# Attention scores of two 64-deep heads: one zero-padded product before, two products on the TensorE array's two halves after

## Chip, cores, metric

The kernel runs on one core of a Trainium2 chip. The metric is the device time of one execution in microseconds (us). A core has five engines: TensorE (PE in the profile; PEld is its weight loads), VectorE (DVE), ScalarE (ACT), GpSimd (POOL) and SyncE (SP), which here only issues DMAs.

## What is computed

Two decoder layers over 256 tokens of width 1024, in float32. Each layer has an attention mixer, a squared-ReLU MLP of hidden width 4096 and a gated embedding. Layer 0 mixes with 8 stick-breaking heads and 4 differential heads (each with two score maps, so also two 64-deep products); layer 1 with 16 heads of block attention, which at 256 tokens is plain causal attention. All heads are 64 deep. Of the scores the reference says, in short:

```
z = einsum('bhqd,bhkd->bhqk', q, k) * scale      # d = 64, q and k: 256 tokens
stick:  w = exp(log_sigmoid(z) + sum of log_sigmoid(-z) over later keys), s < t
diff:   a = softmax(q1 k1) - lam * softmax(q2 k2), causal
layer 1: softmax(q k), causal
```

## The kernel before

Weights stream from HBM. Each unit of 128 x 1024 floats lands in a `raw` buffer, ACT writes its rounded part (`whi`), DVE the rest (`wlo = raw - whi`), and a product of two float32 matrices is three products of the rounded type fp32r: hi x hi, hi x lo, lo x hi (`mm3`). A pair (`whi`, `wlo`) is one of `N_SPLIT` = 6 split buffers, which a chunk gives back when PE has read it. PE works on blocks of 128 tokens (t = 0, 1) by 512 columns, or of 128 columns by 256 tokens (`chunk_T`, `ff1`).

The order of all instructions is written out by a planner in the kernel (class `Order`): tasks are generators with a rank, and the planner picks by rank among those whose inputs are ready by its own clock. The engines then run their lists in order. The trunk (projections, MLP, gate) has rank 80, heads 21 and 22, and the small projection `ple_projection` (products `whi,pT`) has rank 90 and fills in when the trunk has nothing ready; it starts after all scores of its layer (`scored`).

The heads are handled in pairs j of two 64-deep heads, head g on partitions 64g to 64g+63: 4 `stick_pair`, 4 `diff_head`, 8 `moba_pair`. One operand lies in a padded tile (`z` for hi, `zl` for lo) with room for both heads, in which the other head's 64 partitions are zero. A product then contracts over all 128 partitions and yields the scores of both heads side by side. `z_tile` sets the zeros with GpSimd memsets (L1195, L1196): 8 at the start, 4 in layer 1. `qk_sink` and `T_sink` write the two halves of padded tiles with two 64-partition instructions each. For a softmax pair, `soft` computes block t = 0 (128 keys of each head: 256 columns) and later block t = 1 (512 columns). `stick_pair` adds a mask by a bf16 product and sums the logarithms with constants `negl` and `negone`. `average` multiplies by the values in the array's two column halves (`mm_halves`, L165). A head pair holds two of the `N_BIG` = 5 buffers `big` (a stick pair one).

Time is also spent in `transposes` after each residual: transpose on PE, copy by ACT (`tok`), cast and subtraction by DVE (`T0h`, `T0l`), which the next projection reads.

Of the kernel before, what the change touches and what calls it, by code (L numbers as in the profile page):

```python
# [17 lines left out]
P = 128  # L18
# [8 lines left out]
N_SPLIT = 6  # L27
N_RAW = 4
N_BIG = 5
# [11 lines left out]
def width(ap):  # L41
    n = 1
    for s in ap.shape[1:]:
        n *= int(s)
    return n
# [37 lines left out]
class Order:  # L83
# [84 lines left out]

    def transpose(self, out, in_, ident):
        self.nc.tensor.transpose(out, in_, ident)  # L170
        return self.spend("pe", 109)
# [56 lines left out]
def kernel(  # L228
# [25 lines left out]
    NT = 8  # L254
# [348 lines left out]
    def qk_sink(nm, dst, ev, eighth, padded):  # L603
        def sink(t, bk, dep):
            yield (dep, toks.wake, nm.ev[t])
            ti, tok = toks.take()
            rs = nm.rs8 if eighth else nm.rs
            e = o.copy(tok, bk[1], ps=True, scale=rs[:, t:t + 1])
            banks.give(*bk, e)
            yield (e, rope_ev, ropes.wake)  # L610
            ri, r = ropes.take()
            v = tok.rearrange("q (h d) -> q h d", d=64)
            c16 = cc[:, t].rearrange("q a b -> q (a b)").unsqueeze(1).to_broadcast([P, 8, 16])
            o.tt_pool(r[:, 0], v[:, :, 0:16], c16, ALU.mult)
            o.tt_pool(r[:, 1, :, 0:8], v[:, :, 8:16], sn[:, t, 0, :].unsqueeze(1).to_broadcast([P, 8, 8]), ALU.mult)
# [11 lines left out]
            ts_ = slice(t * P, (t + 1) * P)  # L627
# [7 lines left out]
            for v, (hi, lo) in parts:  # L635
                e = o.tt(lo, v, hi.bitcast(F32), ALU.subtract)
            banks.give(bi, ps, e, side=True)
            ev[t].t = e
        return sink
# [15 lines left out]
    def T_sink(dst, evs_, eighth, padded):  # L655
        def sink(f2, bk, dep):
            yield (dep, toks.wake, rsT_ev)
            ti, tok = toks.take()
            v = tok.rearrange("q (j n) -> q j n", j=2)
            ps = bk[1].rearrange("q (j n) -> q j n", j=2)  # L660
            e = o.stt(v, ps, 0.125 if eighth else 1.0, rsT.unsqueeze(1).to_broadcast([P, 2, 256]), ALU.mult, ALU.mult)
            banks.give(*bk, e)
            yield e
            js = slice(2 * f2, 2 * f2 + 2)
            if padded:
                parts = [(v[64 * g:64 * g + 64], [d[64 * g:64 * g + 64, js, g, :] for d in dst]) for g in range(2)]
            else:
                parts = [(v, [d[:, js, :] for d in dst])]
            for v_, (hi, lo) in parts:
                e = o.act(hi, v_, AF.Copy)  # L670
            yield e
            for v_, (hi, lo) in parts:
                e = o.tt(lo, v_, hi.bitcast(F32), ALU.subtract)
            toks.give(ti, tok, e)
            evs_[f2].t = e
        return sink
# [49 lines left out]
    def stick_pair(j, kT, qz, q_ev, k_ev, v, v_ev, acts):  # L726
        yield (q_ev[j // 2], k_ev[j // 2], mask_ev, big.wake)
        b1 = big.take()
        e = b1[1]
        yield lambda: banks.wake(2, side=True)  # L730
        ba, bb = banks.take(side=True), banks.take(side=True)
        pa, pb = ba[1], bb[1][:, :256]
        a3 = pa.rearrange("q (g n) -> q g n", g=2)
        b3 = pb.rearrange("q (g n) -> q g n", g=2)
# [5 lines left out]
        yield ea  # L740
        o.act(e[:, :512], pa, AF.Abs, ps=True)
        o.act(e[:, 512:], pb, AF.Abs, ps=True, dep=eb)
        o.act(e, e, AF.Exp, scale=-1.0)
        t = o.act(e, e, AF.Ln, bias=one)
        yield t
        o.stt(e[:, 512:], pb, 0.0, e[:, 512:], ALU.max, ALU.add)
        t = o.stt(e[:, :512], pa, 0.0, e[:, :512], ALU.max, ALU.add)
# [3 lines left out]
        t = o.act(sph, e, AF.Copy)  # L751
        yield t
        t = o.tt(spl, e, sph.bitcast(F32), ALU.subtract)
# [6 lines left out]
        sps.give(*b2, t2)  # L760
        yield t1
        t1 = o.act(e[:, :512], pa, AF.Exp, ps=True)
        t2 = o.act(e[:, 512:], pb, AF.Exp, ps=True)
        banks.give(*ba, t1, side=True)
        banks.give(*bb, t2, side=True)
        yield (t2, *v_ev)
        wa = e[:, :512].rearrange("q (g n) -> q g n", g=2)
        wb = e[:, 512:].rearrange("q (g n) -> q g n", g=2)
        yield from average(lambda g: wa[:, g, :], lambda g: wb[:, g, :], v, j * P, acts, j, b1)


    def soft(j, t, qT, kz, q_ev, k_ev, e, st):

        n = (t + 1) * P
        yield (q_ev[t], *k_ev[:t + 1], mask_ev)
        yield lambda: banks.wake(side=True)
        bs = banks.take(side=True)
        s3 = bs[1][:, :2 * n].rearrange("q (g k) -> q g k", g=2)
        ts_ = slice(t * P, (t + 1) * P)
        w = mm3(s3, qT[0][:, j, ts_], qT[1][:, j, ts_], kz[0][:, j, :, 0:n], kz[1][:, j, :, 0:n], True, True)  # L780
        if t == 1:
            scored()
        yield w
        for g in range(2):

            nc.vector.tensor_tensor_reduce(e[:, g, :], s3[:, g, :], cmask[:, P * (1 - t):], -1.0, 3.0e38, ALU.add, ALU.min,
                                           accum_out=st[:, g:g + 1])
            w = o.spend("dve", 130 + 1.04 * n)
        banks.give(*bs, w, side=True)
# [9 lines left out]
    def diff_head(j, qT, kz, q_ev, k_ev, v, v_ev, acts):  # L799
# [3 lines left out]
        w = 0.0  # L803
        es = []
        for t in range(2):
            e = be[1][:, 256 * t:256 * t + 256 * (t + 1)].rearrange("q (g k) -> q g k", g=2)
            st = sts[t][1]
            w = yield from soft(j, t, qT, kz, q_ev, k_ev, e, st)
# [42 lines left out]
    def moba_pair(j, jj, qT, kz, q_ev, k_ev, v, v_ev, acts):  # L851
# [4 lines left out]
        aT = ba[1].rearrange("q (g a n) -> q g a n", g=2, a=3)  # L856
        for t in range(2):
# [3 lines left out]
            yield from soft(j, t, qT, kz, q_ev, k_ev, e, st)  # L861
# [327 lines left out]
    def z_tile(name, layer, j):  # L1189

        z = zpool.tile([P, 4, 2, 256], F32R, tag="z", name=name)
        def zeros():
            yield o.now if layer else 1500.0
            for y in (z, zl[j]) if layer == 0 else (z,):
                nc.gpsimd.memset(y[64:128, :, 0, :].bitcast(F32), 0.0)  # L1195
                nc.gpsimd.memset(y[0:64, :, 1, :].bitcast(F32), 0.0)  # L1196
                o.spend("pool", 1800)
        o.add(zeros(), 14)
        return z, zl[j]
# [7 lines left out]
    def trunk():  # L1207
# [6 lines left out]
        for i in range(2):  # L1214
            banks.room[0] += 5 - banks.room[0] if i == 0 else 1
            z = [z_tile(f"z{i}{j}", i, j) for j in range(2)]
# [8 lines left out]
            if i == 0:  # L1225
                o.add(p_task(0, pT_ev, 40000.0), 40)
                sinks = dict(bq=qk_sink(nm, sT[1], evs["bq"], True, False),
                             bk=qk_sink(nm, z[1], evs["bk"], False, True),
                             aq=T_sink(z[0], evs["aq"], True, True),
                             ak=T_sink(sT[0], evs["ak"], False, False),  # L1230
# [10 lines left out]
            else:  # L1241
                o.add(p_task(1, pT_ev, o.now), 40)
                for n, _ in ORDER1:
                    g = int(n[1])
                    s = dict(q=lambda: qk_sink(nm, sT[g], evs[n], True, False),
                             k=lambda: qk_sink(nm, z[g], evs[n], False, True),
# [53 lines left out]
```

## Time and profile before

| | us |
|---|---|
| three runs | 670.27, 670.45, 671.4 (median 670.45) |
| the profiled execution | 671.49, of it 669.7 the span of the trace |
| PE busy | 654.9 |
| DVE, ACT, POOL busy | 450.3, 417.2, 63.8 |

A busy PE is counted from the start of a product to its modelled end. Products overlap, so what one costs is read from the distance to the next, not from its length.

### The profile page before, as it was taken

How to read it: one execution, taken by the hardware profiler on the slowest of the kernel's cores; microseconds unless marked ns; L12 is line 12 of the kernel's file. 1: busy time of each engine (PE TensorE's matmuls, PEld its weight loads, DVE VectorE, ACT ScalarE, POOL GpSimd, SP SyncE). 2: the span in 40 equal slices, each digit the busy share in tenths (PEclk: the TensorE clock that was granted, in tenths of full speed). 3: DMA queues.
4: the chain of work that ended last, by engine and by line, in shares of the span. 5: the costliest groups of instructions: out<-in, count | busy, mean ns of one | idle time of the engine just before them, and what ended most of it. 6: DMA issues, size and time to landing. Idle time of an engine off the chain costs nothing.

```text
span 669.7 us, 10988 instructions
## 1 busy us (share of the span) xinstructions
PE 654.9 (98%) x3906; PEld 572.0 (85%) x3906; DVE 450.3 (67%) x935; ACT 417.2 (62%) x888; POOL 63.8 (10%) x128
## 2 busy tenths in 40 slices
PE   6999999999999999999999999998999999999995
PEld 5899778898998899888888778777998999899885
DVE  6799867766645754577986866747656555655594
ACT  6777986756544644466796767756646543655483
POOL 8650001000000000000052022000000000000010
PEclk9999999999999999999999999999999999999998
DMA  7853733456447544753566434416466546754621
GB/s 255 263 165 106 240 127 112 138 188 213 158 168 252 191 154 159 251 198 120 187 210 187 153 126 136 149 63 189 154 225 218 167 152 218 224 165 156 209 95 63
DMA packets 50054, 115.61 MB, mean 173 GB/s; under 512 B 4000, under 2 KB 5456, under 8 KB 50000
## 3 DMA queue, kind: packets, MB, share of 16 engines
q1 hardware_dynamic: 49824, 114.39, 52.5%
q8 instruction: 30, 0.49, 0.3%
q0 software_dynamic: 176, 0.53, 0.2%
q14 instruction: 24, 0.20, 0.1%
HBM read 113.86 MB, written 1.05 MB: 172 GB/s over the span
## 4 chain that ended last, share of the span: by engine, by line
PE 91%; DVE 3%; POOL 2%; issue 1%; DMA 1%; ACT 1%; SPq 0%; POOLq 0%; DVEq 0%; ACTq 0%
PE bank L159 86%; PE bank L170 3%; DVE wlo L192 2%; PE bank L165 1%; DMA raw<-in_ab_w_in_dram 1%; POOL prod L1110 1%; POOL rem L1111 0%; ACT junk L178 0%; ACT whi L178 0%; DVE h L192 0%; DVE T0h L510 0%; DVE T0l L192 0%; ACT tok L178 0%; POOL negr L312 0%; DVE o L192 0%
## 5 line engine op out<-in xcount | busy, mean ns | idle before, releaser
L192 DVE TENSOR_TENSOR wlo<-raw,whi 128x512 fp32r<-128x512 f32 x424 | 277.1, 694 | 91.4 <-ACT whi L178 65.7
L178 ACT ACTIVATE whi<-raw 128x512 fp32r<-128x512 f32 x424 | 243.7, 626 | 92.7 <-PE bank L159 67.4
L159 PE MATMUL bank<-T0h,whi 128*128 128x256 f32 x576 | 162.8, 283 | 1.7 <-DVE T0h L510 1.7
L159 PE MATMUL bank<-T0h,wlo 128*128 128x256 f32 x576 | 162.3, 282 | 0.3 <-DVE wlo L192 0.2
L159 PE MATMUL bank<-T0l,whi 128*128 128x256 f32 x576 | 162.2, 282 | 0.2
L159 PE MATMUL bank<-whi,hid 128*128 128x512 f32 x512 | 160.9, 390 | 0.0
L159 PEld LDWEIGHTS bank<-whi,hid 128*128 128x128 f32 x512 | 96.1, 188 | 19.2
L159 PEld LDWEIGHTS bank<-T0h,wlo 128*128 128x128 f32 x576 | 110.2, 191 | 0.9 <-DVE wlo L192 0.9
L159 PEld LDWEIGHTS bank<-T0h,whi 128*128 128x128 f32 x576 | 108.3, 188 | 2.8 <-DVE T0h L510 2.1
L159 PEld LDWEIGHTS bank<-T0l,whi 128*128 128x128 f32 x576 | 108.6, 189 | 1.4 <-DVE T0l L192 0.8
L159 PE MATMUL bank<-wlo,hid 128*128 128x512 f32 x256 | 99.6, 389 | 0.0
L192 DVE TENSOR_TENSOR tok<-tok 128x512 f32<-128x512 f32 x32 | 22.1, 690 | 68.3 <-ACT tok L178 68.3
L159 PE MATMUL bank<-whi,T0h 128*128 128x512 f32 x160 | 66.2, 413 | 0.0
L178 ACT ACTIVATE tok<-bank 128x512 f32<-128x512 f32 x32 | 18.8, 586 | 72.4 <-PE bank L159 72.4
L159 PE MATMUL bank<-wlo,T0h 128*128 128x512 f32 x160 | 63.2, 395 | 0.0
L159 PE MATMUL bank<-whi,T0l 128*128 128x512 f32 x160 | 63.1, 394 | 0.0
L159 PEld LDWEIGHTS bank<-wlo,hid 128*128 128x128 f32 x256 | 48.1, 188 | 9.3
L159 PE MATMUL bank<-whi,T1h 128*128 128x512 f32 (+1 forms) x136 | 53.6, 394 | 0.0
L159 PE MATMUL bank<-whi,T1l 128*128 128x512 f32 (+1 forms) x136 | 51.5, 379 | 0.0
L159 PE MATMUL bank<-wlo,T1h 128*128 128x512 f32 (+1 forms) x136 | 51.4, 378 | 0.0
L534 POOL TENSOR_TENSOR rs_p<-ms_p,pexp 128x1 f32<-128x1 f32 x4 | 2.2, 551 | 437.0 <-DVE ms_p L209 437.0
L159 PEld LDWEIGHTS bank<-whi,T0l 128*128 128x128 f32 x160 | 30.3, 190 | 6.6
(159 smaller groups left out, 742.6 us busy)
## 6 DMA issues: line engine op xcount, KB each, us to landing
raw<-in_w_ff_dram SPq DMA_DIRECT2D x128, 512.0 KB, 4.4
raw<-in_moba_w_in_dram SPq DMA_DIRECT2D x24, 512.0 KB, 4.0
raw<-in_ab_w_in_dram SPq DMA_DIRECT2D x23, 512.0 KB, 4.8
raw<-in_ple_gate_dram SPq DMA_DIRECT2D x16, 512.0 KB, 4.7
raw<-in_ab_w_out_dram SPq DMA_DIRECT2D x8, 512.0 KB, 4.1
raw<-in_moba_w_out_dram SPq DMA_DIRECT2D x8, 512.0 KB, 3.3
raw<-in_ple_proj_dram SPq DMA_DIRECT2D x4, 512.0 KB, 3.8
h<-in_x_dram SPq DMA_DIRECT2D x4, 256.0 KB, 5.8
```

The costliest lines, as they stand in the source:

```text
L159: self.nc.tensor.matmul(out, lhsT, rhs, start=start, stop=stop, **kw)
L165: self.nc.tensor.matmul(out, lhsT, rhs, start=start, stop=stop)
L170: self.nc.tensor.transpose(out, in_, ident)
L178: self.nc.scalar.activation(out, in_, func, **kw)
L192: self.nc.vector.tensor_tensor(out, a, b, op=op)
L534: nc.gpsimd.tensor_tensor(nm.rs[:, t:t + 1], b, pexp[:, 0:1], op=ALU.pow)
L1110: nc.gpsimd.tensor_scalar(prod, k, -c, None, op0=ALU.mult)
```

## The change

The padding goes. q and k of a pair lie in unpadded tiles of 128 partitions, and each head's scores are a product over its own 64 partitions, issued alternately for g = 0 and g = 1 into two PSUM banks (`mm3_heads`). For softmax pairs both blocks t are now computed in one go (`scores_of`), into two banks that are held together, and then read by DVE together (`read_scores`). The stick pair's mask and log sums are issued per head. The memsets and the second half of each padded write are gone. Freed room goes to a seventh split buffer, two more `big`, and eight more `tiny`.

```
-N_SPLIT = 6
+N_SPLIT = 7
 N_RAW = 4
-N_BIG = 5
+N_BIG = 7
...
+    def mm3_heads(self, steps, first=True):
+
+        for a, b, start, stop in ((0, 0, first, False), (0, 1, False, False), (1, 0, False, True)):
+            for out, l_, r_ in steps:
+                self.nc.tensor.matmul(out, l_[a], r_[b], start=start, stop=stop, skip_group_check=not first)
...
-    NT = 8
+    NT = 16
...
-            if padded:
-                parts = [(v[64 * g:64 * g + 64], [d[64 * g:64 * g + 64, :, g, ts_] for d in dst]) for g in range(2)]
-            else:
-                parts = [(v, [d[:, :, ts_] for d in dst])]
-            for v, (hi, lo) in parts:
-                e = o.act(hi, v, AF.Copy, ps=True)
+            hi, lo = [d[:, :, t * P:(t + 1) * P] for d in dst]
+            e = o.act(hi, v, AF.Copy, ps=True)
...
+    def head_rows(x, j, g, c0, c1):
+
+        return [d[64 * g:64 * g + 64, j, c0:c1] for d in x]
...
-        mm3(a3, kT[0][:, j, 0:P], kT[1][:, j, 0:P], qz[0][:, j, :, :], qz[1][:, j, :, :], True, False)
-        ea = o.mm(a3[:, :, 0:P], identb, smask, False, True)
-        mm3(b3, kT[0][:, j, P:256], kT[1][:, j, P:256], qz[0][:, j, :, P:256], qz[1][:, j, :, P:256], True, False)
-        eb = o.mm(b3, identb, smask, False, True)
...
+        o.mm3_heads([(ps[g][:, :256], head_rows(kT, j, g, 0, P), head_rows(q, j, g, 0, 256)) for g in range(2)])
+        o.mm3_heads([(ps[g][:, 256:384], head_rows(kT, j, g, P, 256), head_rows(q, j, g, P, 256)) for g in range(2)],
+                    first=False)
+        ws = []
+        for g in range(2):
+            for c in (0, 256):
+                w = o.mm(ps[g][:, c:c + P], identb, smask[:, 0], False, True, skip_group_check=True)
...
-        for s_ in (sph, spl):
-            o.mm(pa, negl, s_[:, :512], False, False, skip_group_check=True)
-            t1 = o.mm(a3[:, :, P:256], negone, s_[:, 512:].rearrange("q (g n) -> q g n", g=2), False, s_ is spl,
-                      skip_group_check=True)
-            t2 = o.mm(pb, negl, s_[:, 512:], False, s_ is spl, skip_group_check=True)
...
+        for g in range(2):
+            for s_ in (sph, spl):
+                sg = s_.rearrange("q (g n) -> q g n", g=2)[:, g]
+                o.mm(ps[g][:, :384], negl, sg, False, False, skip_group_check=True)
+                w = o.mm(ps[g][:, P:256], negone, sg[:, 256:384], False, s_ is spl, skip_group_check=True)
...
+    def scores_of(j, q, k, q_ev, k_ev):
+
+        yield (*q_ev, *k_ev, mask_ev)
+        yield lambda: banks.wake(2, side=True)
+        bs = [banks.take(side=True) for _ in range(2)]
+        ws = [o.mm3_heads([(bs[g][1][:, P * t:P * t + P * (t + 1)], head_rows(q, j, g, P * t, P * (t + 1)),
+                            head_rows(k, j, g, 0, P * (t + 1))) for g in range(2)]) for t in range(2)]
+        scored()
+        return bs, ws
...
-    def z_tile(name, layer, j):
-
-        z = zpool.tile([P, 4, 2, 256], F32R, tag="z", name=name)
-        def zeros():
-            yield o.now if layer else 1500.0
-            for y in (z, zl[j]) if layer == 0 else (z,):
-                nc.gpsimd.memset(y[64:128, :, 0, :].bitcast(F32), 0.0)
-                nc.gpsimd.memset(y[0:64, :, 1, :].bitcast(F32), 0.0)
...
+        z = zpool.tile([P, 2, 4, 256], F32R, tag="z", name=name)
+        return z[:, 0], z[:, 1]
...
-    zl = [cst.tile([P, 4, 2, 256], F32R, name=f"zl{j}") for j in range(2)]
```

## Rows read from the trace of the kernel before

**Rows 1.** The page: span, busy time of engines, and the chain that ended last.
```profile
span 669.7 us, 10988 instructions
PE 654.9 (98%) x3906; PEld 572.0 (85%) x3906; DVE 450.3 (67%) x935; ACT 417.2 (62%) x888; POOL 63.8 (10%) x128
PE 91%; DVE 3%; POOL 2%; issue 1%; DMA 1%; ACT 1%; SPq 0%; POOLq 0%; DVEq 0%; ACTq 0%
```
**Rows 2.** PE in order of time, two softmax pairs (start, length, instruction).
```profile
45.32 0.28 PE L159 MATMUL bank<-z,sT 128*128 128x256 f32 x1
...
46.03 0.28 PE L159 MATMUL bank<-T0h,whi 128*128 128x256 f32 x1
...
48.91 0.40 PE L159 MATMUL bank<-z,sT 128*128 128x512 f32 x1
...
49.61 0.28 PE L159 MATMUL bank<-T0h,whi 128*128 128x256 f32 x1
```
**Rows 3.** PE in order of time, a stick pair's mask and its log sums.
```profile
62.01 0.28 PE L159 MATMUL bank<-smask,identb 128*128 128x256 bf16 x1
...
80.41 0.64 PE L159 MATMUL bank<-sph,negr 128*128 128x512 f32 x3
80.89 0.63 PE L159 MATMUL bank<-spl,negr 128*128 128x512 f32 x3
```
**Rows 4.** PE in order of time, an average in column halves, from three narrow windows.
```profile
81.24 0.28 PE L159 MATMUL bank<-spl,negr 128*128 128x256 f32 x1
81.45 0.44 PE L165 MATMUL bank<-big,v 128*64 128x256 f32 x2
...
81.45 0.65 PE L165 MATMUL bank<-big,v 128*64 128x256 f32 x4
...
81.45 0.87 PE L165 MATMUL bank<-big,v 128*64 128x256 f32 x8
82.25 0.50 PE L159 MATMUL bank<-whi,T0h 128*128 128x512 f32 x1
```
**Rows 5.** Weight loads by line and shape (busy us, mean ns of one).
```profile
L159 PEld LDWEIGHTS bank<-z,sT 128*128 128x128 f32 x32 | 6.1, 190 | 1.4 <-issue 0.5 <-DVE big L209 0.2
L165 PEld LDWEIGHTS bank<-big,v 128*64 128x64 f32 x96 | 5.8, 136 | 5.2 <-issue 1.2 <-ACT whi L178 1.1 <-ACT big L178 0.7
L159 PEld LDWEIGHTS <-identb 128*128 128x128 bf16 x8 | 0.8, 95 | 1.3 <-issue 1.1
```
**Rows 6.** PE in order of time, float32 products of 128 columns.
```profile
99.22 2.17 PE L159 MATMUL bank<-v,big 128*128 128x128 f32 x18
```
**Rows 7.** PE in order of time, first products of layer 1's MLP, with idle time.
```profile
457.64 0.28 PE L159 MATMUL bank<-T0h,whi 128*128 128x256 f32 x1
...
459.93 0.38 PE L159 MATMUL bank<-T0h,whi 128*128 128x256 f32 x1 [1.22 <-DVE T0h L510]
...
463.07 0.28 PE L159 MATMUL bank<-T0h,wlo 128*128 128x256 f32 x1
```
**Rows 8.** DVE in order of time, ahead of that stretch.
```profile
443.95 0.42 DVE L192 TENSOR_TENSOR T1l<-bank,T1h 128x256 fp32r<-128x256 f32 x1 [3.65 <-ACT T1h L178]
```
**Rows 9.** Products that read pT, by stretch: layer 1, then layer 0.
```profile
443.00:446.00 3.00, 2.34 (x9) 1.61 (x9) 0.00 (x0) 0.00 (x0) 1.00 0.04 14
...
127.00:129.50 2.50, 2.04 (x9) 1.69 (x9) 0.00 (x0) 0.00 (x0) 1.00 0.63 176
```
**Rows 10.** The start: GpSimd, then DVE casts by shape, ACT, PE.
```profile
9.63 0.94 POOL L1196 MEMSET zl<- 64x1024 f32 x1
...
L510 DVE CAST T0h<-tok 128x256 fp32r<-128x256 f32 x3 | 2.4, 804 | 0.3 <-ACT tok L178 0.3
...
30.44 0.22 ACT L178 ACTIVATE sh<-rem 128x16 f32<-128x16 f32 x1 [1.28 <-POOL rem L1111]
...
36.87 0.28 PE L159 MATMUL bank<-T0l,whi 128*128 128x256 f32 x1
...
38.27 0.28 PE L159 MATMUL bank<-T0h,whi 128*128 128x256 f32 x1
```

More of the change, by code (lines that the diff above doesn't have):

```diff
@@ L167, in mm_halves @@
         return e
+    def mm3_heads(self, steps, first=True):
+        for a, b, start, stop in ((0, 0, first, False), (0, 1, False, False), (1, 0, False, True)):
+            for out, l_, r_ in steps:
+                self.nc.tensor.matmul(out, l_[a], r_[b], start=start, stop=stop, skip_group_check=not first)
+                e = self.spend("pe", max(0.5 * width(r_[b]) / 2.4, 55.0) + 6)
+        return e
     def transpose(self, out, in_, ident):
@@ L601, with qk_sink @@
     rope_ev = Event()
-    def qk_sink(nm, dst, ev, eighth, padded):
+    def qk_sink(nm, dst, ev, eighth):
         def sink(t, bk, dep):
@@ L626, in sink @@
             v = ps.rearrange("q (j n) -> q j n", j=4)
-            ts_ = slice(t * P, (t + 1) * P)
-            if padded:
-                parts = [(v[64 * g:64 * g + 64], [d[64 * g:64 * g + 64, :, g, ts_] for d in dst]) for g in range(2)]
-            else:
-                parts = [(v, [d[:, :, ts_] for d in dst])]
-            for v, (hi, lo) in parts:
-                e = o.act(hi, v, AF.Copy, ps=True)
+            hi, lo = [d[:, :, t * P:(t + 1) * P] for d in dst]
+            e = o.act(hi, v, AF.Copy, ps=True)
             yield e
-            for v, (hi, lo) in parts:
-                e = o.tt(lo, v, hi.bitcast(F32), ALU.subtract)
+            e = o.tt(lo, v, hi.bitcast(F32), ALU.subtract)
             banks.give(bi, ps, e, side=True)
@@ L653, in rows_task, with T_sink @@
         banks.give(bi, ps, rsT_ev.t, side=True)
-    def T_sink(dst, evs_, eighth, padded):
+    def T_sink(dst, evs_, eighth):
         def sink(f2, bk, dep):
@@ L663, in sink @@
             yield e
[L664 to L670, printed above, removed]
+            hi, lo = [d[:, 2 * f2:2 * f2 + 2, :] for d in dst]
+            e = o.act(hi, v, AF.Copy)
             yield e
-            for v_, (hi, lo) in parts:
-                e = o.tt(lo, v_, hi.bitcast(F32), ALU.subtract)
+            e = o.tt(lo, v, hi.bitcast(F32), ALU.subtract)
             toks.give(ti, tok, e)
@@ L724, in scored, with stick_pair @@
             scores[1].t = o.now
-    def stick_pair(j, kT, qz, q_ev, k_ev, v, v_ev, acts):
+    def head_rows(x, j, g, c0, c1):
+        return [d[64 * g:64 * g + 64, j, c0:c1] for d in x]
+    def stick_pair(j, kT, q, q_ev, k_ev, v, v_ev, acts):
         yield (q_ev[j // 2], k_ev[j // 2], mask_ev, big.wake)
         b1 = big.take()
-        e = b1[1]
+        e = b1[1].rearrange("q (g n) -> q g n", g=2)
         yield lambda: banks.wake(2, side=True)
[L731 to L734, printed above, removed]
-        mm3(a3, kT[0][:, j, 0:P], kT[1][:, j, 0:P], qz[0][:, j, :, :], qz[1][:, j, :, :], True, False)
-        ea = o.mm(a3[:, :, 0:P], identb, smask, False, True)
-        mm3(b3, kT[0][:, j, P:256], kT[1][:, j, P:256], qz[0][:, j, :, P:256], qz[1][:, j, :, P:256], True, False)
-        eb = o.mm(b3, identb, smask, False, True)
-        scored()
[L740 to L744, printed above, removed]
+        bs = [banks.take(side=True) for _ in range(2)]
+        ps = [b[1] for b in bs]
+        o.mm3_heads([(ps[g][:, :256], head_rows(kT, j, g, 0, P), head_rows(q, j, g, 0, 256)) for g in range(2)])
[5 more added lines that the diff above has]
+                w = o.mm(ps[g][:, c:c + P], identb, smask[:, 0], False, True, skip_group_check=True)
+            ws.append(w)
+        scored()
+        yield ws[0]
+        for g in range(2):
+            o.act(e[:, g], ps[g][:, :384], AF.Abs, ps=True, dep=ws[g])
+        o.act(b1[1], b1[1], AF.Exp, scale=-1.0)
+        t = o.act(b1[1], b1[1], AF.Ln, bias=one)
         yield t
-        o.stt(e[:, 512:], pb, 0.0, e[:, 512:], ALU.max, ALU.add)
-        t = o.stt(e[:, :512], pa, 0.0, e[:, :512], ALU.max, ALU.add)
+        for g in range(2):
+            t = o.stt(e[:, g], ps[g][:, :384], 0.0, e[:, g], ALU.max, ALU.add)
         yield (t, sps.wake)
@@ L760, in stick_pair @@
[L760 to L783, printed above, removed]
-        for g in range(2):
[L786 to L789, printed above, removed]
@@ new lines, in stick_pair @@
+        ws = []
+        for g in range(2):
+            for s_ in (sph, spl):
+                sg = s_.rearrange("q (g n) -> q g n", g=2)[:, g]
+                o.mm(ps[g][:, :384], negl, sg, False, False, skip_group_check=True)
+                w = o.mm(ps[g][:, P:256], negone, sg[:, 256:384], False, s_ is spl, skip_group_check=True)
+            ws.append(w)
+        sps.give(*b2, w)
+        yield ws[0]
+        for g in range(2):
+            t = o.act(e[:, g], ps[g][:, :384], AF.Exp, ps=True, dep=ws[g])
+            banks.give(*bs[g], t, side=True)
@@ new lines, in stick_pair, with halves_of @@
+        yield (t, *v_ev)
+        yield from average(lambda g: e[:, g, :256], lambda g: e[:, g, 256:], v, j * P, acts, j, b1)
+    def halves_of(b):
+        return [b[:, 256 * t:256 * t + 256 * (t + 1)].rearrange("q (g k) -> q g k", g=2) for t in range(2)]
+    def scores_of(j, q, k, q_ev, k_ev):
+        yield (*q_ev, *k_ev, mask_ev)
+        yield lambda: banks.wake(2, side=True)
+        bs = [banks.take(side=True) for _ in range(2)]
+        ws = [o.mm3_heads([(bs[g][1][:, P * t:P * t + P * (t + 1)], head_rows(q, j, g, P * t, P * (t + 1)),
+                            head_rows(k, j, g, 0, P * (t + 1))) for g in range(2)]) for t in range(2)]
+        scored()
+        return bs, ws
@@ new lines, in read_scores @@
+    def read_scores(bs, ws, es, sts):
+        yield ws[1]
+        ends = []
+        for t in range(2):
+            n = (t + 1) * P
+            for g in range(2):
+                nc.vector.tensor_tensor_reduce(es[t][:, g, :], bs[g][1][:, P * t:P * t + n], cmask[:, P * (1 - t):], -1.0, 3.0e38,
+                                               ALU.add, ALU.min, accum_out=sts[t][:, g:g + 1])
+                w = o.spend("dve", 130 + 1.04 * n)
+            ends.append(w)
+        for b in bs:
+            banks.give(*b, w, side=True)
+        return ends
@@ L790, in soft @@
+    def soft(w, e, st):
         yield w
@@ L802, in diff_head @@
         sts = [tinies.take(), tinies.take()]
-        w = 0.0
         es = []
+        bs, ws = yield from scores_of(j, qT, kz, q_ev, k_ev)
+        ends = yield from read_scores(bs, ws, halves_of(be[1]), [x[1] for x in sts])
         for t in range(2):
@@ L807, in diff_head @@
             st = sts[t][1]
-            w = yield from soft(j, t, qT, kz, q_ev, k_ev, e, st)
+            w = yield from soft(ends[t], e, st)
             yield lam_ev
@@ L856, in moba_pair @@
         aT = ba[1].rearrange("q (g a n) -> q g a n", g=2, a=3)
+        bs, ws = yield from scores_of(j, qT, kz, q_ev, k_ev)
+        ends = yield from read_scores(bs, ws, halves_of(be[1]), [x[1] for x in sts])
         for t in range(2):
@@ L860, in moba_pair @@
             e = be[1][:, 256 * t:256 * t + n].rearrange("q (g k) -> q g k", g=2)
-            yield from soft(j, t, qT, kz, q_ev, k_ev, e, st)
+            yield from soft(ends[t], e, st)
             for g in range(2):
@@ L1187, in p_task, with z_tile @@
         pT_ev.t = e
-    def z_tile(name, layer, j):
-        z = zpool.tile([P, 4, 2, 256], F32R, tag="z", name=name)
-        def zeros():
-            yield o.now if layer else 1500.0
-            for y in (z, zl[j]) if layer == 0 else (z,):
-                nc.gpsimd.memset(y[64:128, :, 0, :].bitcast(F32), 0.0)
-                nc.gpsimd.memset(y[0:64, :, 1, :].bitcast(F32), 0.0)
-                o.spend("pool", 1800)
-        o.add(zeros(), 14)
-        return z, zl[j]
+    def z_tile(name):
+        z = zpool.tile([P, 2, 4, 256], F32R, tag="z", name=name)
+        return z[:, 0], z[:, 1]
     sl = [cst.tile([P, 4, 256], F32R, name=f"sl{j}") for j in range(2)]
-    zl = [cst.tile([P, 4, 2, 256], F32R, name=f"zl{j}") for j in range(2)]
     cst.tile([P, 80], F32, name="room")
@@ L1215, in trunk @@
             banks.room[0] += 5 - banks.room[0] if i == 0 else 1
-            z = [z_tile(f"z{i}{j}", i, j) for j in range(2)]
+            z = [z_tile(f"z{i}{j}") for j in range(2)]
             v = vpool.tile([P, 2, D], F32, tag="v", name=f"v{i}")
@@ L1226, in trunk @@
                 o.add(p_task(0, pT_ev, 40000.0), 40)
[L1227 to L1230, printed above, removed]
+                sinks = dict(bq=qk_sink(nm, sT[1], evs["bq"], True),
+                             bk=qk_sink(nm, z[1], evs["bk"], False),
+                             aq=T_sink(z[0], evs["aq"], True),
+                             ak=T_sink(sT[0], evs["ak"], False),
                              av=v_sink(nm, v, 0, evs["av"]), bv=v_sink(nm, v, 512, evs["bv"]))
@@ L1244, in trunk @@
                     g = int(n[1])
-                    s = dict(q=lambda: qk_sink(nm, sT[g], evs[n], True, False),
-                             k=lambda: qk_sink(nm, z[g], evs[n], False, True),
+                    s = dict(q=lambda: qk_sink(nm, sT[g], evs[n], True),
+                             k=lambda: qk_sink(nm, z[g], evs[n], False),
                              v=lambda: v_sink(nm, v, 512 * g, evs[n]))[n[0]]()
```

4 lines of the change are left out of this document (2 added, 2 removed).

## The prediction

> **What bounds the kernel now.** I read the page first: PE is busy for 654.9 of 669.7 us and makes 91% of the chain that ended last [rows 1]. The other engines have slack on average, so an edit on DVE, ACT, POOL or in the DMA stream pays only where PE stands still. I then read PE in order of time for what one product costs. Six score products of 256 columns take from 45.32 to 46.03, 0.118 each, and three of 512 columns from 48.91 to 49.61, 0.233 each, to the next product's start [rows 2]. The lengths (0.28 and 0.40) are latency and are not added up. Next, over the same order of time, I looked for places where the distance between products exceeds these prices. After the first 15 us there are few that this change can reach. One is at 457.64 to 463.07, the beginning of layer 1's MLP: 21 products start there, 20 steps that need 2.36 us take 5.43, so 3.1 us are lost, and the row in the middle waits 1.22 for DVE's `T0h` [rows 7]. The other is at 36.87 to 38.27: 5 steps, 0.59 needed, 1.40 taken, 0.8 lost [rows 10]. The reader is to see that everything but PE's own work is worth at most some 5 us here, and that the change moves PE's own work by terms of the same size.
>
> **Softmax pairs, on PE.** There are 12 (4 and 8). Before, a pair costs 3 x 0.118 + 3 x 0.233 = 1.05 us [rows 2]. After, block t = 1 is three duos (one product per half) of 256 columns and block t = 0 three duos of 128. No row before shows row halves; the nearest is `average`, which works in column halves [rows 4]. There the first two products end at 81.89 and the next two at 82.10, so a duo of 256 columns costs 0.21. Those are float32 products, which appear as two records each: nine of 128 columns in the code give 18 records, (2.17 - 0.28) / 17 = 0.111 a record, 0.222 a product [rows 6]. A record of 256 columns alone would be 0.22, so the duo costs what one costs. I take 0.12 for a duo of 256 fp32r columns. Bounds are 0.118 and, without overlap, 0.236.
>
> For a duo of 128 columns the bounds are 0.06, half of 0.118, and 0.222, the float32 price, since fp32r products under 256 columns occur nowhere in the trace. I take 0.11. A weight load of 128 columns lasts 190 ns and one of 64 lasts 136 [rows 5]; 54 ns for 64 columns make some 108 for 128, and each half must load its own, so the duo can hardly come faster, while nothing in the rows asks for the float32 price.
>
> **Going into halves and out again.** Before the average, the last full product ends at 81.24 + 0.28 = 81.52. The first duo ends at 81.89, 0.37 later instead of 0.21. After it, 82.32 is followed by an end at 82.75, 0.43 instead of 0.23 [rows 4]. That is 0.16 in and 0.20 out, 0.36 a visit. The pair's 12 products form one visit, so I add 0.36; the bounds are nothing and 0.36. A pair then costs 3 x 0.12 + 3 x 0.11 + 0.36 = 1.05: the halves win 0.36 and the visit takes it back. Net 0 x 12. The Trainium skill, TensorEngine Tiling (Array Packing), section Key Properties, says that a change of tiling mode, as opposed to a change of tile, drains the engine. The trace agrees for column halves (0.36 a visit), and no run here shows it for row halves. By that rule the sum below stands; without it, it would be 16 x 0.36 lower.
>
> **Stick pairs, on PE.** There are 4. Their score products have the same widths, so again 0. The mask goes from two bf16 products of 256 columns, which are as long as any of that width [rows 3] (0.12 each, 0.24), to four of 128. Their weight load is only 95 ns long [rows 5], so I take 0.07 each between 0.06 and 0.11: 0.28, +0.04. The log sums take 80.89 - 80.41 = 0.48 for one of the two parts [rows 3], 0.95 in all. After, they are four of 384 columns, (0.118 + 0.233) / 2 = 0.175 each, and four of 128 at 0.11: 1.14, +0.19. Together +0.23 x 4 = +0.9 us. PE's work thus grows by 0.9. Its low bound is no visit cost (-5.8) and 128 columns at 0.06 (48 duos and 16 products, 64 x -0.05 = -3.2, masks -0.2): -8.3. Its high bound is 128 columns at 0.222 (64 x 0.11 = +7.2) and masks at 0.11 (+0.6): +8.7.
>
> **The stall at 457.64.** DVE makes the last `T0h` and `T0l` there between splits of weights, and PE waits [rows 7]. Two edits bear on it. A seventh split buffer lets one more unit be split earlier: DVE stands idle 3.65 us before 443.95 [rows 8], with the split buffers full. That takes two `wlo` of about 0.68, 1.3 us, out of the crowded stretch. Second, 9 of layer 1's 24 `pT` products were spent at 443 to 446, while the trunk waited for the last heads; in layer 0 such a batch of nine comes only at 127 to 129.5, beside the norm [rows 9], and no PE gap follows it. Seven `big` let three pairs run at once instead of two, and a pair's blocks are scored together, so the last heads end earlier, and those nine, 9 x 0.23 = 2.0 us, are left over for the norm. Both together exceed 3.1. I take 2.5, bounds 0 and 3.1.
>
> **The stall at 36.87.** ACT waited 1.28 us for GpSimd's rotary tables at 30.44 with weight splits queued behind it, and PE's weights came late after that [rows 10]. Eight memsets of about 0.95 us, the last at 9.63, stood ahead of the tables. Without them the tables come some us earlier. I take the whole 0.8, bound 0. **The start.** Between 5 and 11 us three casts by DVE beside those memsets took 2.4 us in all [rows 10]. PE's first products follow them, but most of the start waits for weights. I take 0.5 between 0 and 1.4.
>
> **What costs nothing.** The padded writes drop from two instructions to one: less ACT and DVE work, hidden behind PE outside the stalls above. DVE now reads all four score blocks at once and holds two banks; what queues behind are weight splits, and these are covered by full split buffers (the idle time of rows 8). Without that cover it costs up to the two extra reads, under 1 us a pair. No DMA is added; a seventh buffer brings each load forward by a unit at most.
>
> **The sum.** +0.9 - 2.5 - 0.8 - 0.5 = -2.9 us. The profiled execution took 671.49, of it 669.7 span; it would be 668.6. It is 1.04 above the median of the three runs, so against the median, 670.45 - 2.9 = 667.5 us. I count as no change what lies within 0.2%, 1.3 us, about what a measurement here can tell.
>
> **Rivals.**
> - *A visit to row halves costs nothing.* Weight loads for the other rows may run ahead where those for the other columns did not. For it: only the rows are divided, and the output columns stay. Against it: the one visit that the trace shows is paid both ways [rows 4]. Then -5.8 more: 661.7 us.
> - *fp32r products of 128 columns run at the float32 price* (0.222, [rows 6]). For it: the kernel before has no fp32r product under 256 columns. Place: block t = 0 of every pair and the stick pairs' second blocks and `negone`, 64 x 0.11 = +7.2, so 674.7 us, slower. It decides from 0.18 a product on: (2.9 + 1.3) / 64 = 0.066 above 0.11.
> - *The halves do not overlap*, so that the change does not do what it says: duos cost 0.236 and 0.22 instead of 0.12 and 0.11, +0.68 x 16 = +11, so 678.5 us. Column halves overlap [rows 4], which speaks against it. The Trainium skill, TensorE: Matmul & The Clock Gate, Part 3, gives 3.07 times for four row tiles; no run here shows that.
> - *The stall at 457.64 stays*, since the planner's order is new and DVE may again have splits ahead of the last casts. Then 2.5 is missing: 670.0 us, no change.
>
> **Chances.** The forecast has 0.48: the visit is seen on the same array and the weight load bounds the narrow products. Of that, 0.40 is faster, 0.07 within 0.2% and 0.01 slower, as the stalls give between nothing and 5. The free visit has 0.20 (faster), the float32 price 0.12 (slower), no overlap 0.05 (slower), the stall that stays 0.15 (0.10 same, 0.05 slower). Faster 0.60, same 0.17, slower 0.23. The forecast's own range is 665 to 670. The range from 660.5 to 673.5 takes in the free visit and the lasting stall and leaves out the float32 price and no overlap, 0.17, and some tails.
>
> **What the profile after would show.** Products of 64 rows should start in twos a few ns apart; the duos at 0.12 and 0.11, and the end of the first full product after a visit some 0.2 late. The start of layer 1's MLP should run without a DVE wait, with all 24 `pT` products close to it, and the first stretch should have no ACT wait on GpSimd. The prediction is wrong if duos of 128 columns are spaced at 0.2 or more, if visits show no late ends, or if PE gaps of over 1 us turn up inside the attention stages, where none are now.

## The result, and the profile after

The kernel after the change takes 663.99 us (median of four runs, 663.65 to 664.14) against 670.92 for the kernel before in the same comparison: ratio 0.9895 [0.9883, 0.9907], 6.9 us faster. The forecast was faster, by 2.9. The profiled execution of after took 663.65, with a span of 661.9 against 669.7 [rows 1]. The trace of before is of one of its longer executions (671.49), so the two traces lie 7.8 us apart and the medians 6.9; sums over the traces below add up to 7.8.

The page of after: span, busy time of engines, the chain that ended last.
```profile
span 661.9 us, 11160 instructions
PE 648.1 (98%) x4018; PEld 569.5 (86%) x4018; DVE 443.3 (67%) x930; ACT 410.1 (62%) x877; POOL 53.0 (8%) x116
PE 92%; POOL 2%; DVE 2%; issue 1%; DMA 1%; ACT 1%; SPq 0%; POOLq 0%; DVEq 0%; ACTq 0%
```
PE has 112 instructions more and is busy 6.8 us less. PE is still nearly the whole chain, so the saving must be in PE's own order of time.

After, PE in order of time, from windows of several widths (a row gathers like products as far as its window reaches): the first stretch with a gap, a stick pair's log sums and scores with an average behind, the fourth stick pair's scores, three pairs of layer 1 in one go, averages, the beginning of layer 1's MLP.
```profile
36.62 0.28 PE L159 MATMUL bank<-T0l,whi 128*128 128x256 f32 x1
37.07 0.39 PE L159 MATMUL bank<-T0h,wlo 128*128 128x256 f32 x1 [0.17 <-DVE wlo L200]
...
79.58 0.45 PE L159 MATMUL bank<-spl,negr 128*128 128x384 f32 x2
79.87 0.45 PE L159 MATMUL bank<-sph,negr 128*128 128x384 f32 x2
...
81.17 0.27 PE L173 MATMUL bank<-z,sl 64*128 64x128 f32 x2
81.37 0.40 PE L159 MATMUL bank<-smask,identb 128*128 128x128 bf16 x4
81.70 0.87 PE L165 MATMUL bank<-big,v 128*64 128x256 f32 x8
...
86.62 0.51 PE L173 MATMUL bank<-z,sT 64*128 64x256 f32 x4
...
365.72 0.40 PE L159 MATMUL bank<-whi,T0l 128*128 128x512 f32 x1
366.05 0.33 PE L173 MATMUL bank<-z,sT 64*128 64x128 f32 x2
...
366.84 0.33 PE L173 MATMUL bank<-z,sT 64*128 64x128 f32 x4
...
367.53 0.34 PE L173 MATMUL bank<-z,sT 64*128 64x128 f32 x4
...
368.10 0.28 PE L173 MATMUL bank<-z,sl 64*128 64x256 f32 x2
368.30 0.50 PE L159 MATMUL bank<-whi,T0h 128*128 128x512 f32 x1
...
422.98 2.17 PE L165 MATMUL bank<-big,v 128*64 128x256 f32 x24
...
452.89 0.28 PE L159 MATMUL bank<-T0h,whi 128*128 128x256 f32 x1
...
454.54 0.28 PE L159 MATMUL bank<-T0h,wlo 128*128 128x256 f32 x1
```
In the middle is what the sum missed. The last full product ends at 366.12, then three pairs follow without a full product between them, 0.69 from pair to pair (366.84, 367.53). The last of their 36 products ends at 368.38: 2.26 us, 0.19 more than three times 0.69, which is the way in. The next full product ends 0.42 later, where 0.23 is its price: 0.20 for the way out. The three pairs go into halves once, and cost 2.45 together, 0.82 each instead of 1.05 [rows 2]. The averages gather as well, 24 records in a row at 422.98 where before eight stood alone [rows 4].

I call a stretch of half-array products between two full ones a visit. For the whole span I added up the distances between the ends of successive PE instructions, by what the instruction is. A full product of 256 columns counts as 0.118 and one of 512 as 0.227; what comes late behind half-array products is "the way out", and other lateness over 0.06 is a gap (that of products at a low granted clock too).

| us | before | after |
|---|---|---|
| score products, with the way in | 17.56 | 12.76 |
| averages, with the way in | 9.61 | 9.16 |
| the way out (another 0.77 stands with the scores before) | 1.64 | 2.42 |
| mask and log sums | 4.78 | 5.71 |
| gaps | 9.16 | 4.77 |
| visits for scores / for averages | 0 / 12 | 10 / 9 |

So PE's own work, all rows but the gaps, shrank by 3.5 (forecast: +0.9), and the gaps by 4.4 (forecast: 3.8). The ten visits of after are 36, 12, 36, 12, 36 and 12 products for the softmax pairs, and four of 12 for the stick pairs.

### The profile page after: what moved, and what is told of

It is laid out like the page before. It is cut to its first block, busy times and chain, and to the rows that moved or that the text cites. A ratio compares the mean times of both kernels' runs of the same rounds, so it can differ in the third digit from the quotient of the medians.

```text
span 661.9 us, 11160 instructions
## 1 busy us (share of the span) xinstructions
PE 648.1 (98%) x4018; PEld 569.5 (86%) x4018; DVE 443.3 (67%) x930; ACT 410.1 (62%) x877; POOL 53.0 (8%) x116
## 3 DMA queue, kind: packets, MB, share of 16 engines
HBM read 113.86 MB, written 1.05 MB: 174 GB/s over the span
## 4 chain that ended last, share of the span: by engine, by line
PE 92%; POOL 2%; DVE 2%; issue 1%; DMA 1%; ACT 1%; SPq 0%; POOLq 0%; DVEq 0%; ACTq 0%
PE bank L159 86%; PE bank L178 3%; PE bank L173 2%; PE bank L165 1%; DMA raw<-in_ab_w_in_dram 1%; DVE wlo L200 1%; POOL prod L1127 1%; POOL rem L1128 0%; ACT junk L186 0%; ACT whi L186 0%; ACT tok L186 0%; DVE o L200 0%; DVE cc L217 0%; SPq L407 0%; SPq L277 0%
## 5 line engine op out<-in xcount | busy, mean ns | idle before, releaser
L159 PEld LDWEIGHTS bank<-whi,T0h 128*128 128x128 f32 x160 | 30.3, 189 | 8.2 <-ACT whi L186 1.4
```

Source lines behind the costliest of these rows:

```text
L159: self.nc.tensor.matmul(out, lhsT, rhs, start=start, stop=stop, **kw)
```

## The experiments

Each changes the kernel after, and was timed beside the kernel before (the ratios are to it); differences below are against 663.99 unless said otherwise.

**Which buffers matter.** Three runs set buffers back: **big5** N_BIG alone, **split6** N_SPLIT alone, and **scores_only** all three.

```
 big5:        N_BIG = 7 -> 5
 split6:      N_SPLIT = 7 -> 6
 scores_only: N_BIG = 7 -> 5, N_SPLIT = 7 -> 6, NT = 16 -> 8
```


> The changed kernel with 5 big buffers instead of 7, so two pairs in flight instead of three. Theory A (the visits to array halves are shared): with two pairs in flight the softmax pairs come alone or in twos; each visit more than the 6 of the changed kernel costs 0.4 us, so up to 6 more visits for scores and 3 more for averages, +2 to +3.6 us, and the last heads end later, so the stall at the start of layer 1's MLP comes back in part, +1 to +3: 667 to 670.5 us. Theory B (the duos of products are cheap by themselves, and the buffers matter by the stall alone): 665 to 667 us with the number of PE's gaps in the attention stages unchanged.

> The changed kernel with 6 split buffers as before instead of 7. If the seventh split buffer removed the stall at the start of layer 1's MLP by taking weight splits out of the crowded stretch, 1 to 1.5 us come back there: 665 to 665.5 us. If the earlier end of the heads removed it, the time stays at 664 us and the gap stays away.

> The change without the new buffers: 6 split buffers, 5 big, 8 tiny as before, scores in halves, both blocks at once, no memsets. Theory A (the last heads end earlier because both blocks are scored in one go, which alone keeps the stall at the start of layer 1's MLP away; buffers only share visits): about as with 5 big, 665 to 666 us. Theory B (either kind of new buffer is enough to remove that stall, and without both it is back): 667.5 to 669 us with DVE waits of 2 to 3 us at about 455.

Measured: big5 665.40 (0.9917 [0.9905, 0.993]), split6 664.68 (0.9904 [0.9889, 0.9918]), scores_only 676.04 (1.0078 [1.0066, 1.009]). The change without its buffers is thus slower than the kernel before, by 5. Its PE order of time shows where:
```profile
62.12 0.44 PE L173 MATMUL bank<-z,sT 64*128 64x128 f32 x4
...
99.73 0.40 PE L159 MATMUL bank<-whi,T1l 128*128 128x512 f32 x1
102.82 0.44 PE L178 MATMUL bank<-ident,o 128*128 128x128 f32 x2 [2.69 <-DVE T1l L200]
...
106.81 0.50 PE L173 MATMUL bank<-z,sT 64*128 64x256 f32 x4
...
140.22 0.58 PE L159 MATMUL bank<-T0h,whi 128*128 128x256 f32 x1 [2.62 <-DVE T0h L518]
```
The widths tell the pairs apart: a stick pair begins with 256 columns, a softmax pair with 128. At 62.12 the fourth differential pair is scored, ahead of all stick pairs. Each differential pair keeps a `big` until its values come at about 93 us, so four of them leave one of five to the stick pairs. The fourth stick pair is scored at 106.81; in after at 86.62. While the trunk waits for these late heads PE runs out of products: it stands still for 2.69 us up to 102.82, and spends 21 of layer 0's 24 `pT` products ahead of time, so that they are missing beside the norm, where PE waits 2.62 up to 140.22. Products that read `pT`:
```profile
106.00:122.00 16.00, 5.71 (x21) 3.78 (x21) 0.00 (x0) 0.00 (x0) 1.00 0.28 98
```
In all it has 16.1 us of gaps against 4.8; some 2.4 of them are late products at a granted clock of 0.50, behind the second wait.

In big5, with five `big` too, PE takes three differential pairs and then a stick pair:
```profile
55.13 0.44 PE L173 MATMUL bank<-z,sT 64*128 64x128 f32 x4
...
62.24 0.51 PE L173 MATMUL bank<-z,sT 64*128 64x256 f32 x4
```
So the planner's order decides whether five are short. big5 differs from scores_only by seven split buffers and 16 `tiny`; which of the two turns the order was not tried. **late4** tests whether that order makes the gaps: scores_only, with the fourth differential pair held until the stick keys are there.

```
+    def diff_head(j, ..., late):
+        if j == 3:
+            yield late                     # evs["ak"][1]
```


> The run without the new buffers (676 us), with one edit: the fourth differential pair starts only when the keys of the stick pairs are there. Theory A (it took the two buffers that two stick pairs need, and kept one to the end): 665.5 to 667.5 us, gaps at 103 and 137 to 141 us gone. Theory B (the gaps come from fewer split buffers or another part of the order): 673 to 676 us.

Measured: 666.14 (0.993 [0.9917, 0.9943]), 9.9 less than scores_only, and 6.3 us of gaps. The fourth stick pair now comes at 84.64:
```profile
84.64 0.50 PE L173 MATMUL bank<-z,sT 64*128 64x256 f32 x4
```
So the fourth differential pair's place makes up 9.9 of the 12.0 us by which scores_only is longer than after. Two runs asked how many buffers are worth having: **big7** keeps the seven `big` alone, **big9** goes on to nine.

```
 big7: N_SPLIT = 6, NT = 8, N_BIG = 7
 big9: N_SPLIT = 6, N_BIG = 9
```


> The change with 7 big buffers, but 6 split buffers and 8 tiny as before. Theory A (of the new buffers the big ones do it: the four differential pairs hold one each until the values arrive, and with 5 the stick pairs are left with one): 664 to 665 us, with no gap over 1 us after 40 us. Theory B (tiny or split buffers matter as well): 667 to 676 us.

> The changed kernel with 6 split and 9 big buffers, which fit in the same room. If more pairs in flight share more visits, up to 3 visits of 0.4 us each are saved: 662.8 to 664 us. If the banks limit what comes together, 664 to 664.7 us as with 6 split buffers.

Measured: big7 663.72 (0.9894 [0.988, 0.9908]), big9 665.36 (0.9917 [0.9902, 0.9931]). With seven `big`, the split buffer and the `tiny` buffers are worth nothing that can be measured; beyond seven nothing is won. What the two more `big` are worth where five don't jam shows in big5: its softmax pairs come in twos at most, 24 products a visit, with 13 visits for scores and 11 for averages instead of 10 and 9, and it takes 1.4 us more (0.7 of it in scores, averages and ways out).

**What the halves alone are worth.** In **full**, the softmax pairs' scores go back to full-array products, both blocks still in one go; **full_big5** also has five `big`.

```
-        ws = [o.mm3_heads(...) for t in range(2)]
+        for t in range(2):
+            s3 = bs[t][1][:, :2 * n].rearrange("q (g k) -> q g k", g=2)
+            ws.append(mm3(s3, q[0][:, j, P*t:n], ..., k[0][:, j0:j0+2, 0:n], ...))
```


> The changed kernel, all its buffers and order, but the scores of the softmax pairs are computed by full-array products of the old widths (256 and 512 columns over 128 partitions); their values mix neighbouring heads, so the output is not the reference's, and only the time is looked at. Theory A: 12 pairs cost 12.6 us instead of 12 x 0.69 + 6 visits x 0.4 = 10.7 us, so +1.9: about 666 us. Theory B (duos cheap, visits free): 12 x (1.05 - 0.69) = +4.3: about 668.3 us. Theory C (the halves give nothing, all of the gain comes from the buffers and the memsets): 664 us.

> As the run with full-array scores of the softmax pairs (their values mix neighbouring heads), with 5 big buffers instead of 7. Theory A: without visits for the softmax pairs the buffers are worth only the averages' visits and the stall, +1 to +3 against the full-array run; and against 5 big with halves it is about equal, within 1.3 us, since unshared visits take back what the duos win. Theory B: it is 4 us slower than 5 big with halves.

Measured: full 667.86 (0.996 [0.9946, 0.9973]), 3.9 more than after; full_big5 675.39 (1.0064 [1.0051, 1.0077]). In full the scores, averages and ways out add up to 27.8 against 24.3 in after, and the gaps to 5.2 against 4.8: 3.4 of the 3.9 are PE's work. The result is nearer to the larger of the two sums expected, the one with free visits. The smaller one had left out that shared scores gather the averages too: full has 12 visits for averages instead of nine. Against before, full has the same PE work (33.6 us with masks and log sums in both) and 3.9 less in gaps. So roughly 3.9 of the 6.9 us that after wins come from the halves, and the rest from gaps that go without them. The price does not need halves to show: both blocks in one go with five `big` jam here too (four differential pairs from 45.87 to 61, the first stick pair at 71.67, 14.6 us of gaps).

**What a visit costs.** **apart** adds one small full-array product behind each softmax pair, so that no two pairs share a visit. **together** adds the same product on 64 rows, which leaves PE in halves. In both, the added product is written onto the first block's scores of one head; only the time is read from these two runs.

```
+    nought = cst.tile([P, P], BF16, name="nought")        # zeros
+        ws[1] = o.mm(bs[0][1][:, 0:P], identb, nought, ...)   # together: identb[0:64], nought[0:64]
```


> The changed kernel with one small full-array product (bf16, 128 columns, of a tile of zeros) after each softmax pair's 12 half-array products, so that no two pairs share a visit. Theory A (a visit costs some 0.35 us, and the changed kernel makes few since pairs come together): 12 x 0.06 for the products, and 6 further visits of 0.2 in and 0.1 out, +2.5: about 666.5 us. Theory B (visits cost nothing that the next products do not hide; the duos win all): 664.7 us, as with the half-array product.

> As the run before it in this set, with the small product on 64 rows, so that it stays within the halves: the control. Both theories: 12 x 0.06 = +0.7, about 664.7 us.

Measured: apart 666.50 (0.9934 [0.9922, 0.9947]), together 665.18 (0.9916 [0.9903, 0.9929]). First apart, PE in order of time, three pairs of layer 1:
```profile
367.23 0.44 PE L173 MATMUL bank<-z,sT 64*128 64x128 f32 x4
...
368.12 0.23 PE L159 MATMUL bank<-nought,identb 128*128 128x128 bf16 x1
368.28 0.44 PE L173 MATMUL bank<-z,sT 64*128 64x128 f32 x4
...
369.17 0.23 PE L159 MATMUL bank<-nought,identb 128*128 128x128 bf16 x1
369.32 0.44 PE L173 MATMUL bank<-z,sT 64*128 64x128 f32 x4
```
And together, the added products of three pairs:
```profile
367.44 0.23 PE L159 MATMUL bank<-nought,identb 64*128 64x128 bf16 x1
...
368.25 0.23 PE L159 MATMUL bank<-nought,identb 64*128 64x128 bf16 x1
...
369.06 0.23 PE L159 MATMUL bank<-nought,identb 64*128 64x128 bf16 x1
```
From pair to pair it is 1.05 apart (367.23 to 368.28) and 0.81 together (367.44 to 368.25): 0.24 a visit, in and out. Six more visits (16 instead of 10) make 1.3 us in the runs, 0.22 each (1.8 in all had been expected). That is less than the 0.36 of column halves; the product behind these visits is the small bf16 one, and ahead of a full fp32r product the way out alone is 0.20.

**Both blocks in one go.** **byblock** scores and reads the blocks of a pair one after the other, as before the change, but in halves and with the new buffers. **byblock_old** is the same with the old numbers of buffers.

```
-    def scores_of(j, q, k, q_ev, k_ev):
+    def scores_of(j, t, q, k, q_ev, k_ev):
-        ws = [o.mm3_heads([...]) for t in range(2)]
+        w = o.mm3_heads([...])             # block t; then read_scores(t, ...), soft
 byblock_old: also N_SPLIT = 6, N_BIG = 5, NT = 8
```


> The changed kernel with the two blocks of a softmax pair scored one after the other, as before, each with its own 6 half-array products, read and softmax; all buffers stay. Theory A (scoring both blocks in one go is what shares visits and ends the heads early): up to 24 block visits instead of 6, of which several still come together, +2 to +4 us, and the gap at the start of layer 1's MLP is back with 1 to 3 us: 667 to 671 us. Theory B (buffers do both): 664 to 665 us and no gap.

> The run with the two blocks scored one after the other, now also with 6 split buffers, 5 big and 8 tiny as before: of the change only the half-array products and the missing memsets and double writes are left. Theory A (the last heads of layer 1 end early either by three pairs in flight or by both blocks in one go; without either, products that read pT are spent before 450 us and the gap at the start of layer 1's MLP is back): 24 visits, PE's work 2 us over that of before, a gap of 2 to 3 us at about 460: 671 to 673.5 us, or more if the fourth differential pair again keeps the stick pairs waiting. Theory B (missing memsets and double writes removed the gap): no DVE wait over 1 us after 450 us, 669 to 671 us.

Measured: byblock 671.09 (1.0003 [0.9994, 1.0012]), byblock_old 670.31 (0.999 [0.9981, 0.9999]). In byblock, PE in order of time, a first block between full products and a second one:
```profile
369.64 0.40 PE L159 MATMUL bank<-whi,T0l 128*128 128x512 f32 x1
369.96 0.44 PE L173 MATMUL bank<-z,sT 64*128 64x128 f32 x4
...
370.45 0.50 PE L159 MATMUL bank<-whi,T0h 128*128 128x512 f32 x1
...
375.86 0.40 PE L159 MATMUL bank<-whi,T0l 128*128 128x512 f32 x1
376.19 0.50 PE L173 MATMUL bank<-z,sT 64*128 64x256 f32 x4
...
376.74 0.50 PE L159 MATMUL bank<-whi,T0h 128*128 128x512 f32 x1
```
From the end at 370.04 to the end at 370.95 it is 0.91, less 0.23 for the full product 0.68; for the second block 377.24 - 376.26 - 0.23 = 0.75. A pair in two visits so costs 1.43, more than the 1.05 of full products. There are 24 visits instead of 10, and scores and ways out add up to 20.5 against 15.2: 5.3 of the 8.1 by which its span is longer than after's, with 2.3 more in gaps. Of the 5.3, 0.9 is one wait inside the first visit, up to 46.28; the other 4.4 are 0.31 for each of the 14 visits more.

| us | blocks one after the other | both in one go |
|---|---|---|
| 5 `big`, 6 split, 8 `tiny` | 670.3 | 676.0 (666.1 with the fourth pair held) |
| 7 `big`, 7 split, 16 `tiny` | 671.1 | 664.0 |

With the blocks one after the other, halves change nothing, be the buffers old or new. Only with both blocks in one go do few visits come about, and the buffers keep that from jamming.

**The memsets.** **memsets** puts the zeroing by GpSimd back, onto tiles that don't need it.

```
+            for w in range(1 if layer else 2):
+                nc.gpsimd.memset(z[64:128, w].bitcast(F32), 0.0)
+                nc.gpsimd.memset(z[0:64, w].bitcast(F32), 0.0)
```


> The changed kernel with the memsets put back on GpSimd (8 at the start, 4 in layer 1, of 64 x 1024 each, on tiles that are written afterwards). If they held up the rotary tables and the first casts, 0.5 to 1.3 us come back before 40 us: 664.5 to 665.3 us. If they were hidden, 664 us.

Measured: 664.70 (0.9908 [0.9895, 0.992]), 0.7 more, about half of what a measurement can tell from nothing. First DVE's casts between 5 and 11 us by shape, in memsets and in after, then ACT in order of time in after:
```profile
L518 DVE CAST T0h<-tok 128x256 fp32r<-128x256 f32 x3 | 2.6, 866 | 0.3 <-ACT tok L186 0.3
...
L518 DVE CAST T0h<-tok 128x256 fp32r<-128x256 f32 x4 | 1.2, 290 | 0.3 <-ACT tok L186 0.3
...
29.51 0.21 ACT L186 ACTIVATE sh<-rem 128x16 f32<-128x16 f32 x1 [1.28 <-POOL rem L1128]
```
So the memsets do slow the casts, from 290 to 866 ns, but ACT's wait for GpSimd is there without them too. The gaps of memsets are 6.1 against 4.8. At 37 us 0.9 is lost against 0.43 in after; but the other twelve runs, all without memsets, lose 0.5 to 0.8 there, so that this is not clear of their scatter.

## Why the prediction was wrong

**The step that failed** is "The pair's 12 products form one visit, so I add 0.36". It put one visit beside each of 16 pairs and left the 12 visits of the averages as they were: 28. There are 19. The paragraph on the stall itself said that three pairs would run at once, but the sum for the visits was not made with that. In numbers: 28 visits x 0.36 = 10.1 were forecast. In after, scores, averages and ways out are 24.34. Pairs without visits are 16 x 0.686 = 11.0. The averages without theirs are 7.7 (before: 9.61 less 12 x 0.16 for the way in). What is left, 5.7, is 19 visits at 0.30. Nine fewer at 0.36 make 3.2, and 19 cheaper by 0.06 make 1.1, together the 4.4 by which PE's own work came out below the forecast. That pairs sharing a visit save time was shown by apart and together, and that many visits undo the change by byblock. (The medians, 4.0 apart from the forecast, show a little less than the traces, with 4.4 here and 0.6 in the gaps.)

**Prices that were right.** A pair costs 0.686 beside the forecast 3 x 0.12 + 3 x 0.11 = 0.69. Weight loads for the halves last as long as full ones [rows 5]:
```profile
L173 PEld LDWEIGHTS bank<-z,sT 64*128 64x128 f32 x128 | 9.7, 186 | 2.1 <-issue 0.9 <-ACT whi L186 0.7
```
The two loads of a duo start together, and duo follows duo at 0.11 to 0.12 whether 128 or 256 columns wide. This agrees with the argument from the loads, and rules out the rivals of the float32 price and of no overlap. The free visit is out too, by the 0.20 behind the visit at 368.30. The Trainium skill, TensorEngine Tiling (Array Packing), section Key Properties, has a change of tiling mode drain the engine; the trace now agrees for row halves, 0.20 in and 0.20 out. Log sums and masks grew by 0.9 together, as forecast, but in part by luck: from end to end the products of 384 columns take 0.17 to 0.23 instead of 0.175, those of 128 take 0.06 instead of 0.11, and the first mask product holds the way out, which the forecast had put with the pair.

**The stall at 457.64** went wholly: 3.1, the forecast's upper bound, where it took 2.5. The 14 steps from 452.89 to 454.54 take 0.118 each, and there is no wait for DVE. Of the nine early `pT` products three are left, at 438.8; the others come after 446. After, products that read `pT` by stretch:
```profile
443.00:446.00 3.00, 0.00 (x0) 0.00 (x0) 0.00 (x0) 0.00 (x0) 1.00 0.00 0
446.00:453.00 7.00, 5.41 (x21) 3.79 (x21) 0.00 (x0) 0.00 (x0) 1.00 0.52 154
```
No run brought the stall back in layer 1: not six split buffers, not five `big`, not the memsets, not the blocks one after the other. So split6 speaks against the forecast's first reason, the seventh split buffer (its only trace there is one product 0.35 late). But stalls of the same kind turn up at the beginning of layer 0's MLP, as in byblock_old (products that read `pT`, then PE in order of time):
```profile
119.00:124.00 5.00, 3.15 (x12) 2.18 (x12) 0.00 (x0) 0.00 (x0) 1.00 0.33 119
...
136.07 0.38 PE L159 MATMUL bank<-T0h,whi 128*128 128x256 f32 x1 [1.39 <-DVE T0h L518]
```
In the 15 traces an MLP begins 30 times. Four beginnings lose 2 us or more, and they are the four with nine or more `pT` products spent over 9 us ahead of them: before in layer 1 (nine early, 3.1 lost), and in layer 0 byblock_old (12, 2.0), full_big5 (21, 3.4) and scores_only (21, 5.5), the last two in part at a granted clock of 0.50. With three early ones or none, at most 0.35 is lost; and full_big5 has its stall with seven split buffers. That bears out the forecast's second reason, the products left over beside the norm, and not the first, though no run changed their place alone. Which edit moved them in layer 1 stays open, since the planner's order is made anew by any edit.

**The stall at 36.87** lost 0.4 of its 0.8. The forecast was that ACT would no longer wait for the tables: it still waits 1.28, at 29.51 instead of 30.44 [rows 10], so its mechanism failed, and even the 0.4 is hardly clear of the 0.5 to 0.8 that the other runs lose there.

**The start** gave 0.6 in these two traces, near its 0.5, but the runs do not bear that out, so it is luck. PE's products have the same order in both there. The 29th ends at 14.28 before, 14.15 in memsets, 12.00 after and 12.1 to 13.4 in the others, as the casts are three times shorter. But then PE waits for weights from ACT and DVE: the 31st ends at 14.80 before, 14.85 in memsets, 14.17 after and 14.0 to 15.1 in the others. The gaps' total of 4.4 is then 3.1, 0.4 and 0.6, with 0.25 at 53.6.

**Gaps inside the attention stages**, which the prediction named as a sign of its failure, did turn up where five `big` jammed, in scores_only and full_big5. That the new `big` keep the new order from jamming, and are not only a bonus for it, it did not see.

## What to carry to other kernels

When products switch an array's mode, count the switches in the order in which they will run, not the products: here 24 visits gave no gain and 10 gave 1%. Work that is fused into one go takes its buffers earlier and holds them longer, so try it together with more of them and look for who keeps one while waiting for something late. Where a planner rewrites the whole order at each edit, a gap that vanishes cannot be put down to one edit without runs that bring it back; then compare all places of its kind in all traces, and look for what the long gaps share.

## What the runs showed of the hardware

The way out of halves depends on what follows: 0.20 before an fp32r product of 512 columns, 0.11 before the bf16 mask at 81.37 (the 0.24 for in and out together in apart fits this).

A gap can cost twice. In full_big5, PE in order of time, then windows of 3 us (time, busy time of PE, PEld, DVE, ACT and POOL, granted clock, DMA):
```profile
102.36 0.44 PE L178 MATMUL bank<-ident,o 128*128 128x128 f32 x2 [2.02 <-DVE T1l L200]
...
100.00:103.00 3.00, 0.98 (x6) 0.59 (x5) 2.36 (x7) 3.00 (x6) 0.00 (x0) 1.00 0.00 0
103.00:106.00 3.00, 3.00 (x10) 2.33 (x9) 2.55 (x5) 0.89 (x3) 0.00 (x0) 0.51 0.03 5
106.00:109.00 3.00, 3.00 (x28) 2.61 (x27) 0.38 (x1) 1.26 (x3) 0.00 (x0) 0.92 0.58 175
```
PE stood still for 2.02 us up to 102.36. In the window that begins at 103 the granted clock was 0.51, the lower of two levels (1.2 instead of 2.4 GHz), and products of 512 columns came 0.43 apart instead of 0.23, which cost some 1.4 us more. In scores_only two longer gaps ended differently, here the windows behind the one at 102.82 (2.69) and the one at 140.22 (2.62):
```profile
103.00:106.00 3.00, 3.00 (x18) 2.57 (x18) 2.91 (x6) 1.35 (x3) 0.00 (x0) 1.00 0.00 0
...
141.00:144.00 3.00, 3.00 (x15) 3.00 (x15) 2.86 (x10) 2.10 (x5) 0.00 (x0) 0.50 0.71 231
```
So the length of one gap alone does not tell whether the clock will fall.
